# Odd heads' probabilities scaled on GpSimd, and TensorE's queue in the attention ordered by a new model of the engines

## The chip, the cores and the metric

The kernel runs on one core of one Trainium2 chip. The metric is the device time of one execution in microseconds (us); lower is better. A core has TensorE (PE, matrix products), VectorE (DVE), ScalarE (ACT), GpSimd (POOL) and SyncE (SP, which issues most of the transfers here). Each engine executes its own queue in order, and engines wait for one another through semaphores.

## The reference

One decoder layer over 1024 tokens with a width of 1024: RMS norm, one input projection, two token mixers side by side (sparse attention and gated linear attention), a gated merge, an output projection, and a SwiGLU feed-forward block. The change lies in the attention mixer, which does this for each block of 128 queries, each of 8 heads (2 groups of 4):

```python
p_c = masked_softmax(sc, cmp_end[None, :] <= t[:, None])          # compressed keys, 63 of them
o_c = jnp.einsum('bghqn,bgnd->bghqd', p_c.astype(v_cmp.dtype), v_cmp)
...
p_s = masked_softmax(ss, m_s)                                     # selected blocks
o_s = jnp.einsum('bghqm,bgqmd->bghqd', p_s.astype(vs.dtype), vs)
...
p_w = masked_softmax(sw, m_w)                                     # window of 512 tokens
o_w = jnp.einsum('bghqk,bgkd->bghqd', p_w.astype(vwin.dtype), vwin)
gt = lax.dynamic_slice_in_dim(gates, s, Q_BLOCK, axis=3)
return gt[..., 0:1] * o_c + gt[..., 1:2] * o_s + gt[..., 2:3] * o_w
```

With 16 blocks of 64 tokens and 16 selected, every valid block is selected, so the selected branch is causal attention over all earlier tokens.

## The kernel before

**Work of the attention.** A *unit* is one group and one block of 128 queries: first group 0 with i = 7 down to 0, then group 1 with i = 0 up to 7. A unit has two pairs of heads (j = 0, 1). For each pair there is a selected branch (br = 1, `nkb` = i + 1 blocks of 128 keys) and a window branch (br = 2, at most 5 blocks); the compressed branch (br = 0) serves all four heads of the unit at once. The two heads of a pair are called `par` 0 (even) and 1 (odd).

A branch goes through three kinds of steps on TensorE:

- *Scores* (S): products of queries and keys into a PSUM tile `s` (two buffers). DVE adds the mask, writes the probabilities' tile `p` to SBUF (four buffers) and finds the row's extreme (`masked`, line 1135). ACT takes the exponential and sums it (line 1174 for one head, 1162 for a pair). `weigh` then takes the reciprocal of the sum (line 1141) and multiplies `p` by it and by the branch's gate, so that the three branches can be added up in one accumulation. With up to `PAIR` = 4 blocks the two heads are done in one step (`pair_scores`), with more in one step each (`head_scores`).
- *Turns* (T): TensorE transposes up to two blocks of both heads into the PSUM tile `t` (two buffers, line 1210). ACT copies it as the high part `pth` (line 1187), and DVE subtracts that for the low part `ptl` (line 1188).
- *Values* (P): products of both parts with the values into the PSUM tile `o` (line 1219). After a unit's last, `finish` copies the two halves out and adds them on POOL (line 1239).

In `weigh` the even head is scaled on DVE by the reciprocal and the gate in one instruction (line 1149). For the odd head DVE first multiplies reciprocal and gate, 128x1 (line 1146), and ACT then scales `p` (line 1147).

`unit` prepares a unit's rotated queries: a load of the rope table, two shuffles on DVE (1069), three products on POOL (1070 to 1072), four transfers through SP, a copy on ACT (1081) and a subtraction on POOL (1082).

**Fill.** Beside the attention TensorE has independent work, single matmuls of 512 columns (line 431, tile `d`, one PSUM buffer): 14 column tiles of the gate projection, two halves of 24 matmuls each, and 5 tiles of an up-projection, two halves of 12. After a half's last matmul DVE (line 969) or ACT (line 1255) evacuates it. Its weights come from transfers on SP, are split by ACT (372) and POOL (373).

**Order.** TensorE's queue is written out in program order. In the attention `Plan.run` decides that order while the program is built: it keeps a time `t` for TensorE and estimates of when ACT (A), DVE (D) and POOL (P) will be done, and takes at each point a turn, a score or a value step that it holds to be ready, in this order of preference, or else an item of fill. The order of the instructions on the other engines is chosen by the scheduler of the language, from its own simulation. In the old planner each engine has one free time, `on` adds a step to it in the order of the calls, and fill is taken only if nothing of the attention becomes ready within `WAIT` = 300 ns:

```python
if self.fill.q and self.d <= self.t and nxt[0] > self.t + WAIT:
    cost, fn = self.fill.q.popleft()
```

After the plan, what fill is left is issued, and the merge of the two mixers follows (its sigmoid is line 1344).

Of the kernel before, what the change touches and what calls it, by code (L numbers as in the profile page):

```python
# [14 lines left out]
AF = mybir.ActivationFunctionType  # L15
OP = mybir.AluOpType
AX = mybir.AxisListType.X

T, D, DFF = 1024, 1024, 2816
# [86 lines left out]


PAIR, PMAX, PREP = 4, 3, 3
LAT, WAIT, LOADED, COPIED = 155.0, 300.0, 1500.0, 3000.0
NBIG, NMID, NSMALL = 18, 10, 8  # L110
SCRATCH = 2048
FINE, NGATE, AHEAD = 3, 2, 1200

UP = (1, 2, 4, 5, 7)


class Plan:

    def __init__(self, brs, fill, unit):
        self.fill, self.unit = fill, unit
        self.t, self.free = 0.0, dict(A=0.0, D=0.0, P=0.0)
        self.s, self.tb = [0.0] * 2, [0.0] * 2
        self.p = [0.0] * 4
        self.o = self.d = 0.0
        self.turns, self.pend = deque(), deque()
        self.scores = deque()
        self.prep = deque()
        self.known = {}  # L130
        seen = None
        for b in brs:
            if (b.g, b.i) != seen:
                seen = (b.g, b.i)
                self.prep.append((*seen, len(self.scores)))
            for fn, n in b.scores():
                self.scores.append((b, fn, n))
            b.ready = None
            ts = b.turns()
            for k, (fn, n) in enumerate(ts):  # L140
                self.turns.append((b, fn, n, k == len(ts) - 1))
        n = len(self.scores)
        self.prep = deque((g, i, n - k) for g, i, k in self.prep)

    def on(self, eng, ready, dur):
        self.free[eng] = max(self.free[eng], ready + LAT) + dur
        return self.free[eng]

    def prepare(self):
        u = self.prep.popleft()[:2]  # L150
        self.unit(*u)
        t = self.on("D", self.t, 600.0)
        t = self.on("P", t, 2300.0)
        t = self.on("A", t + COPIED, 600.0)
        self.known[u] = self.on("P", t, 1300.0)

    def score_at(self):

        if not self.scores:
            return None  # L160
        b, fn, n = self.scores[0]
        u = (b.g, b.i)
        if self.prep and len(self.scores) <= self.prep[0][2] + PREP:
            self.prepare()
        held = 0 if b.br == 0 else 1
        if len(self.p) < held:
            return None
        return max(self.s[0], self.known[u] if b.br else 0.0)

    def score(self):  # L170
        b, fn, n = self.scores.popleft()
        fn()
        w = 64 if b.br == 0 else 128 * b.nkb
        if b.br == 0:
            cost = 540.0
        else:
            cost = n * 2 * max(107.0, w / 2.4)
        self.t += cost
        self.s.pop(0)
        pf = self.p.pop(0) if b.br else 0.0  # L180
        m = n if b.br else 4
        t = self.on("D", max(self.t, pf), 65 * m + 1.041 * w * m)
        u, t = t, self.on("A", t, m * (237 + 0.833 * w))
        self.s.append((u if b.br else t) + LAT)
        self.s.sort()
        t = self.on("D", t, 150.0)
        t = max(self.on("D", t, 130 + 0.52 * w if b.br else 330.0), self.on("A", t, 187 + 0.833 * w) if b.br and n == 2 else 0.0)
        b.ready = max(b.ready or 0.0, t + LAT)
        b.left = getattr(b, "left", 2) - n

    def turn_at(self):
        if not self.turns or len(self.pend) >= PMAX:
            return None
        b = self.turns[0][0]
        if getattr(b, "left", 2):
            return None
        return max(b.ready, self.tb[0])

    def turn(self):
        b, fn, n, last = self.turns.popleft()  # L200
        later = fn()
        self.t += 218.0 * n
        self.tb.pop(0)
        t = self.on("A", self.t, 50 + 214.0 * n)
        t = self.on("D", t, 68 + 267.0 * n)
        self.tb.append(t + LAT)
        self.tb.sort()
        self.pend.append((t + LAT, later, n, b, last))
        if last and b.br:
            self.p += [self.t + LAT] * (1 if b.nkb <= PAIR else 2)  # L210

    def value_at(self):
        if not self.pend:
            return None
        t, _, _, b, _ = self.pend[0]
        return max(t, self.o) if b.br == 0 and b.j == 0 else t

    def value(self):
        _, later, n, b, last = self.pend.popleft()
        later()  # L220
        self.t += 218.0 * n if b.br else 436.0
        if last and b.br == 2 and b.j == 1:
            self.o = max(self.on("A", self.t, 478.0), self.on("D", self.t, 550.0)) + LAT

    def run(self):
        ops = dict(T=(self.turn_at, self.turn), S=(self.score_at, self.score), P=(self.value_at, self.value))
        while self.scores or self.turns or self.pend:
            at = {k: ops[k][0]() for k in ops}
            now = [k for k in ops if at[k] is not None and at[k] <= self.t]
            if now:  # L230
                ops[now[0]][1]()
                continue
            nxt = min((v, k) for k, v in at.items() if v is not None)
            if self.fill.q and self.d <= self.t and nxt[0] > self.t + WAIT:
                cost, fn = self.fill.q.popleft()
                self.t += cost
                said = fn()
                if said == "pause":
                    self.d = self.on("D", self.t, 670.0) + LAT
                elif said in ("part", "load"):  # L240
                    self.d = self.t + (LOADED if said == "load" else LOADED / 2)
                    self.on("A", self.t + 2500.0, 1040.0)
                continue
            self.t = nxt[0] if not self.fill.q or nxt[0] <= self.t + WAIT else min(nxt[0], self.d)


@with_exitstack
def layer_kernel(ctx, tc, a, outT):
# [135 lines left out]
    def dense(jobs, two=True, per=1, ready=None):  # L384

        w, out = dict(ready or {}), []
        todo = deque((n, o) for n, job in enumerate(jobs) for o in range(0, job[0].shape[1], 4) if (n, o) not in w)
        raw = deque()  # L390

        def fetch():
            if todo:
                n, o = todo.popleft()
                raw.append(((n, o), raw_half(jobs[n][0], o)))

        def load():
            if not raw:
                fetch()
            if raw:  # L400
                at, t = raw.popleft()
                w[at] = half_parts(*t)
            fetch()

        def at(n):
            def getw(k):
                wh, wl = w[n, k // 4 * 4]
                return wh[:, k % 4, :], wl[:, k % 4, :]
            return getw

        out += [(0.0, load if i >= len(w) else lambda: None) for i in range(3)]
        for n in range(len(jobs)):
            items = jobs[n][1](at(n))
            if jobs[n][0].shape[1] > 4:
                cut = (len(items) // 2 if two else 0) + 4 * per
                out += items[:cut] + [(0.0, load)] + items[cut:]
            else:
                out += items
            out.append((0.0, load))
        return out  # L420

    def products(getw, bank, xh, xl, w0, evac, fine=False):

        st, out, n = {}, [], len(xh)

        def at(k, i):
            if k + i == 0:
                st["p"] = bank()
            wh, wl = getw(w0 + k)
            w, x = ((wh, xh[k]), (wh, xl[k]), (wl, xh[k]))[i]  # L430
            PE.matmul(st["p"], w, x, start=k + i == 0, stop=k == n - 1 and i == 2)  # L431
            if k == n - 1 and i == 2:
                evac(st["p"])
                return "pause"

        for k in range(n):
            if fine:
                out += [(216.0, lambda k=k, i=i: at(k, i)) for i in range(3)]
            else:
                out.append((648.0, lambda k=k: [at(k, i) for i in range(3)][2]))  # L440
        return out
# [643 lines left out]
    class Branch:  # L1085
# [51 lines left out]
        def weigh(self, pars, ps, z):  # L1137
# [4 lines left out]
            for i, par in reversed(list(enumerate(pars))):  # L1142
                p, ri, gi = ps[i], r[:, i:i + 1], UN[self.g, self.i]["gt"][:, self.br, h + i:h + i + 1]
                self.p[par] = p
                if par:
                    V.tensor_mul(ri, ri, gi)
                    S.activation(p, p, AF.Copy, scale=ri)
                else:
                    V.tensor_scalar(p, p, ri, gi, op0=OP.mult, op1=OP.mult)

        def pair_scores(self):

# [223 lines left out]
    last = []  # L1376
# [574 lines left out]
```

## Time and profile before

| | |
|---|---|
| time, median of 3 runs | 1565.43 us (1564.54 to 1568.66) |
| the profiled execution | 1564.79 us, span 1563.0 us |
| TensorE, matmul busy | 1542.0 us (99% of the span) |
| DVE / ACT / POOL busy | 1014.2 / 813.0 / 720.4 us (65 / 52 / 46%) |
| granted TensorE clock, mean | 0.998 |
| attention, from the first scores to the last values | about 361 to 762 us |

Busy time is the union of an engine's instructions. Matmuls are pipelined and their ends are modelled, so a short wait of TensorE can lie under the modelled end of the matmul before it; the start times of neighbours show it. A group's row reads: line, engine, operation, tiles written and read, shapes, count | busy us, mean ns of one | idle us of the engine before them, and what ended it. A row of waits reads: who waited <- for whom: us in total, times, longest.

### The profile page before, as it was taken

What the parts mean: (1) busy time and instruction counts of PE and PEld (TensorE: products, weight loads), DVE (VectorE), ACT (ScalarE), POOL (GpSimd) and SP (SyncE); (2) the same over time, 40 slices, a digit from 0 to 9 for tenths busy, and PEclk for the clock granted to TensorE, in tenths of its full rate; (3) what the DMA queues carried; (4) which work ended last, traced back from release to release, by engine and by line L of the source; (5) the groups of instructions that cost most, each with busy time, mean ns of one, the idle gap of its engine ahead of it and who ended that gap; (6) DMA issues with size and microseconds to landing.
All of it is one profiled execution on the core that took longest, in us unless ns stands there. A gap on an engine that the chain in (4) does not pass through costs nothing.

```text
span 1563.0 us, 22871 instructions
## 1 busy us (share of the span) xinstructions
PE 1542.0 (99%) x7871; PEld 1309.6 (84%) x7871; DVE 1014.2 (65%) x1788; ACT 813.0 (52%) x1615; POOL 720.4 (46%) x635
## 2 busy tenths in 40 slices
PE   9999999999999999999999999999999999999998
PEld 7888988888888888888888888888888888888887
DVE  7781487586787778777574677544444444599785
ACT  6241555575776767687653454334333334454542
POOL 6110366573223353343256510666666666555570
PEclk9999999999999999999999999999999999999999
DMA  5431212332111222221656621322222323885422
GB/s 180 139 105 55 69 51 65 119 108 78 48 58 55 77 87 72 85 88 61 200 169 229 197 88 68 121 101 102 101 101 102 101 101 108 299 320 163 141 88 108
DMA packets 109944, 180.15 MB, mean 115 GB/s; under 512 B 13426, under 2 KB 30595, under 8 KB 109828
## 3 DMA queue, kind: packets, MB, share of 16 engines
q1 hardware_dynamic: 105796, 172.25, 33.4%
q10 hardware_dynamic: 4032, 6.44, 1.1%
q8 instruction: 62, 1.02, 0.3%
q14 instruction: 54, 0.44, 0.1%
HBM read 128.57 MB, written 45.88 MB: 112 GB/s over the span
## 4 chain that ended last, share of the span: by engine, by line
PE 93%; DVE 3%; ACT 1%; issue 1%; POOL 0%; DVEq 0%; POOLq 0%; ACTq 0%
PE m L431 19%; PE d L431 11%; PE m L1494 9%; PE m L1492 9%; PE m L1493 9%; PE m L1880 5%; PE m L1882 4%; PE m L1881 4%; PE t L1210 3%; PE o L1219 3%; PE s L1130 2%; PE s L1129 2%; PE t L749 2%; PE t L750 1%; PE t L751 1%; PE t L884 1%
## 5 line engine op out<-in xcount | busy, mean ns | idle before, releaser
L373 POOL TENSOR_TENSOR wl<-wf,wh 128x512 fp32r<-128x512 f32 x106 | 146.5, 1389 | 260.7 <-ACT wh L372 237.4
L1492 PE MATMUL m<-xt,wh 128*128 128x512 f32 x412 | 160.3, 389 | 0.0
L1493 PE MATMUL m<-xt,wh 128*128 128x512 f32 x412 | 160.3, 389 | 0.0
L1494 PE MATMUL m<-xt,wl 128*128 128x512 f32 x412 | 160.3, 389 | 0.0
L1409 POOL TENSOR_TENSOR wl<-ws,wh 128x512 fp32r<-128x512 f32 x76 | 107.6, 1420 | 73.3 <-ACT wh L1408 73.3
L1188 DVE TENSOR_TENSOR ptl<-t,pth 128x512 fp32r<-128x512 f32 (+1 forms) x168 | 99.2, 597 | 42.7 <-ACT pth L1187 40.5
L1409 POOL TENSOR_TENSOR wl<-wr,wh 128x512 fp32r<-128x512 f32 x69 | 92.0, 1333 | 70.3 <-ACT wh L1408 69.3
L1408 ACT ACTIVATE wh<-wr 128x512 fp32r<-128x512 f32 x87 | 55.0, 632 | 121.3 <-POOL wl L1409 89.1
L1408 ACT ACTIVATE wh<-ws 128x512 fp32r<-128x512 f32 x76 | 48.0, 632 | 131.4 <-PE m L1493 113.8
L1187 ACT ACTIVATE pth<-t 128x512 fp32r<-128x512 f32 (+1 forms) x168 | 86.4, 519 | 53.0 <-PE t L1210 43.7
L1880 PE MATMUL m<-xb,wh 128*128 128x512 f32 x280 | 109.1, 389 | 0.3 <-DVE g L1554 0.3
L1409 POOL TENSOR_TENSOR wl<-wd,wh 128x512 fp32r<-128x512 f32 x56 | 81.9, 1465 | 59.1 <-ACT wh L1408 57.7
L1881 PE MATMUL m<-xb,wh 128*128 128x512 f32 x280 | 109.0, 389 | 0.0
L1882 PE MATMUL m<-xb,wl 128*128 128x512 f32 x280 | 108.9, 389 | 0.0
L1409 DVE TENSOR_TENSOR xb<-ar,xb 128x512 fp32r<-128x512 f32 x73 | 82.3, 1146 | 29.0 <-ACT xb L1408 29.0
L431 PE MATMUL m<-hh,wh 128*128 128x512 f32 x240 | 99.9, 416 | 0.1
L372 ACT ACTIVATE wh<-wf 128x512 fp32r<-128x512 f32 x106 | 66.1, 626 | 61.1 <-PE m L431 19.9
L1135 DVE CUSTOM_DVE_ANT_0 p<-s,qz 128x640 f32<-128x640 f32 (+7 forms) x128 | 86.3, 700 | 12.8 <-PE s L1130 12.5
L431 PE MATMUL m<-hh,wl 128*128 128x512 f32 x240 | 93.8, 391 | 0.0
L431 PE MATMUL m<-hl,wh 128*128 128x512 f32 x240 | 93.6, 390 | 0.0
L1210 PE MATMUL t<-ident,p 128*128 128x128 f32 x528 | 83.9, 275 | 8.4 <-DVE ptl L1188 6.1
L1493 PEld LDWEIGHTS m<-xt,wh 128*128 128x128 f32 x412 | 77.4, 188 | 16.2
(402 smaller groups left out, 4506.4 us busy)
## 6 DMA issues: line engine op xcount, KB each, us to landing
ar<-actd SPq DMA_DIRECT2D x77, 256.0 KB, 2.8
wf<-in_w_t SPq DMA_DIRECT2D x58, 256.0 KB, 2.8
wr<-in_w_gate SPq DMA_DIRECT2D x44, 256.0 KB, 2.8
wr<-in_w_upf SPq DMA_DIRECT2D x44, 256.0 KB, 2.7
wd<-in_w_down SPq DMA_DIRECT2D x33, 256.0 KB, 5.2
zd<-zt SPq DMA_DIRECT2D x32, 256.0 KB, 2.0
zz<-zd SPq DMA_DIRECT2D x16, 512.0 KB, 4.7
wf<-in_w_out SPq DMA_DIRECT2D x32, 256.0 KB, 3.3
```

Of the source, the lines that this page charges most:

```text
L373: P.tensor_tensor(tl, wf, f(th), OP.subtract)
L431: PE.matmul(st["p"], w, x, start=k + i == 0, stop=k == n - 1 and i == 2)
L1188: V.tensor_tensor(tl[:, :c], pt[:, :c], f(th[:, :c]), OP.subtract)
L1210: PE.transpose(pt[:, bs(2 * b + par)], self.p[par][:, bs(kb + b)], ident)
L1408: S.activation(th, src, AF.Copy)
L1409: eng.tensor_tensor(tl, src, f(th), OP.subtract)
L1492: PE.matmul(ps, wh[:, c], xh, start=first and k == 0, stop=False, skip_group_check=not first)
L1493: PE.matmul(ps, wh[:, c], xl, start=False, stop=False, skip_group_check=not first)
L1494: PE.matmul(ps, wl[:, c], xh, start=False, stop=k == MH - 1, skip_group_check=not first)
L1880: PE.matmul(dst, wh[:, c], xh, start=first and p == 0, stop=False, skip_group_check=not first)
L1881: PE.matmul(dst, wh[:, c], xl, start=False, stop=False, skip_group_check=not first)
L1882: PE.matmul(dst, wl[:, c], xh, start=False, stop=p == NP - 1, skip_group_check=not first)
```

## The change

Two things. In `weigh`, the odd head's probabilities are multiplied by reciprocal and gate in one instruction on POOL, with the same form that the even head has on DVE; ACT's scaling and DVE's small product are gone. And `Plan` has a new model: every instruction group of ACT, DVE and POOL is a `Step` with predecessors; `advance` runs each engine's waiting steps, the earliest issued of those that are ready first; `over` tells whether a step has ended by now. Its durations are new, steps of a pair are counted one head at a time, and loads of weights put work on ACT and POOL. Fill is taken as soon as no attention step is ready, and a group of fill with fewer than `CLOSE` = 6 matmuls left goes ahead of the attention.

```diff
-LAT, WAIT, LOADED, COPIED = 155.0, 300.0, 1500.0, 3000.0
+LAT, TAIL, LOADED, COPIED = 100.0, 320.0, 1500.0, 3000.0
+CLOSE = 6
...
-    def on(self, eng, ready, dur):
-        self.free[eng] = max(self.free[eng], ready + LAT) + dur
-        return self.free[eng]
+    def step(self, eng, dur, *after, lag=LAT):
+        self.n += 1
+        s = Step(dur, 0.0, self.n)
+        for x in after:
+            if not isinstance(x, Step):
+                s.at = max(s.at, x + lag)
+            elif x.end is not None:
+                s.at = max(s.at, x.end + lag)
+            else:
+                x.outs.append((s, lag, eng))
+                s.left += 1
+        if not s.left:
+            self.wait[eng].append(s)
+        return s
+
+    def advance(self, t):
+        while True:
+            best = None
+            for e, w in self.wait.items():
+                if w:
+                    at = max(self.free[e], min(s.at for s in w))
+                    if at < t and (best is None or at < best[0]):
+                        best = at, e
+            if best is None:
+                return
+            at, e = best
+            s = min((s for s in self.wait[e] if s.at <= at), key=lambda s: s.seq)
+            self.wait[e].remove(s)
+            s.end = self.free[e] = at + s.dur
+            for x, lag, eng in s.outs:
+                x.at, x.left = max(x.at, s.end + lag), x.left - 1
+                if not x.left:
+                    self.wait[eng].append(x)
+
+    def over(self, x):
+        if isinstance(x, Step):
+            return x.end is not None and x.end + LAT <= self.t
+        return x <= self.t
...
     def score(self):
...
-        m = n if b.br else 4
-        t = self.on("D", max(self.t, pf), 65 * m + 1.041 * w * m)
-        u, t = t, self.on("A", t, m * (237 + 0.833 * w))
-        self.s.append((u if b.br else t) + LAT)
-        self.s.sort()
-        t = self.on("D", t, 150.0)
-        t = max(self.on("D", t, 130 + 0.52 * w if b.br else 330.0), self.on("A", t, 187 + 0.833 * w) if b.br and n == 2 else 0.0)
...
+            m = [self.step("D", 232.0 + 1.043 * w, self.t, pf, lag=TAIL) for _ in range(n)]
+            self.s.append(m[-1])
+            zs = [self.step("A", 469.0 + 0.851 * w, x) for x in m]
+            r = self.step("D", 160.0, *zs)
+            par = getattr(b, "par", 0)
+            if n == 2 or par:
+                b.steps.append(self.step("P", 100.0 + 1.05 * w, r))
+            if n == 2 or not par:
+                b.steps.append(self.step("D", 270.0 + 0.53 * w, r, lag=0.0))
+            b.par = par + 1
...
     def turn(self):
...
-        t = self.on("A", self.t, 50 + 214.0 * n)
-        t = self.on("D", t, 68 + 267.0 * n)
+        t = self.step("A", 165.0 + 214.0 * n, self.t, lag=TAIL)
+        t = self.step("D", 151.0 + 268.0 * n, t)
...
     def run(self):
...
+            self.advance(self.t)
+            now = next((do for ok, do in ops if ok()), None)
+            if now and not (self.fill.q and getattr(self.fill.q[0][1], "left", CLOSE) < CLOSE and self.over(self.d)):
+                now()
                 continue
-            nxt = min((v, k) for k, v in at.items() if v is not None)
-            if self.fill.q and self.d <= self.t and nxt[0] > self.t + WAIT:
+            if self.fill.q and self.over(self.d):
                 cost, fn = self.fill.q.popleft()
                 self.t += cost
                 said = fn()
...
+                elif said == "weights":
+                    self.step("P", 1292.0, self.step("A", 630.0, self.t + 2500.0))
...
-            self.t = nxt[0] if not self.fill.q or nxt[0] <= self.t + WAIT else min(nxt[0], self.d)
+            self.t += 25.0
...
-                if par:
-                    V.tensor_mul(ri, ri, gi)
-                    S.activation(p, p, AF.Copy, scale=ri)
-                else:
-                    V.tensor_scalar(p, p, ri, gi, op0=OP.mult, op1=OP.mult)
+                (P if par else V).tensor_scalar(p, p, ri, gi, op0=OP.mult, op1=OP.mult)
```

More of the change, by code (lines that the diff above doesn't have):

```diff
@@ L108, with __init__ @@
 PAIR, PMAX, PREP = 4, 3, 3
-LAT, WAIT, LOADED, COPIED = 155.0, 300.0, 1500.0, 3000.0
+LAT, TAIL, LOADED, COPIED = 100.0, 320.0, 1500.0, 3000.0
 NBIG, NMID, NSMALL = 18, 10, 8
 SCRATCH = 2048
+CLOSE = 6
 FINE, NGATE, AHEAD = 3, 2, 1200
 UP = (1, 2, 4, 5, 7)
+class Step:
+    __slots__ = ("dur", "left", "at", "outs", "end", "seq")
+    def __init__(self, dur, at, seq):
+        self.dur, self.at, self.seq = dur, at, seq
+        self.left, self.outs, self.end = 0, [], None
 class Plan:
@@ L122, in __init__ @@
         self.fill, self.unit = fill, unit
-        self.t, self.free = 0.0, dict(A=0.0, D=0.0, P=0.0)
+        self.t, self.n = 0.0, 0
+        self.free, self.wait = dict(A=0.0, D=0.0, P=0.0), dict(A=[], D=[], P=[])
         self.s, self.tb = [0.0] * 2, [0.0] * 2
@@ L137, in __init__ @@
                 self.scores.append((b, fn, n))
-            b.ready = None
+            b.steps, b.left = [], 2
             ts = b.turns()
@@ L151, in prepare, with score_now @@
         self.unit(*u)
[L152 to L157, printed above, removed]
+        t = self.step("D", 600.0, self.t)
+        t = self.step("P", 2230.0, t)
+        t = self.step("A", 630.0, t, lag=COPIED)
+        self.known[u] = self.step("P", 1295.0, t)
+    def score_now(self):
         if not self.scores:
-            return None
+            return False
         b, fn, n = self.scores[0]
@@ L164, in score_at @@
             self.prepare()
[L165 to L168, printed above, removed]
+        if len(self.p) < (0 if b.br == 0 else 1):
+            return False
+        return any(self.over(x) for x in self.s) and (not b.br or self.over(self.known[u]))
     def score(self):
@@ L173, in score, with turn_now @@
         w = 64 if b.br == 0 else 128 * b.nkb
+        self.t += 540.0 if b.br == 0 else n * 2 * max(108.0, w / 2.4 + 13)
+        self.s.remove(next(x for x in self.s if self.over(x)))
         if b.br == 0:
-            cost = 540.0
-        else:
[L177 to L180, printed above, removed]
-        m = n if b.br else 4
-        t = self.on("D", max(self.t, pf), 65 * m + 1.041 * w * m)
-        u, t = t, self.on("A", t, m * (237 + 0.833 * w))
-        self.s.append((u if b.br else t) + LAT)
-        self.s.sort()
-        t = self.on("D", t, 150.0)
-        t = max(self.on("D", t, 130 + 0.52 * w if b.br else 330.0), self.on("A", t, 187 + 0.833 * w) if b.br and n == 2 else 0.0)
-        b.ready = max(b.ready or 0.0, t + LAT)
-        b.left = getattr(b, "left", 2) - n
-    def turn_at(self):
+            t = self.step("D", 414.0, self.t, lag=TAIL)
+            e = self.step("A", 2056.0, t)
+            self.s.append(e)
+            t = self.step("D", 178.0, e)
+            t = self.step("D", 446.0, t, lag=0.0)
+            b.steps.append(self.step("D", 426.0, t, lag=0.0))
+        else:
+            pf, zs = self.p.pop(0), []
+            m = [self.step("D", 232.0 + 1.043 * w, self.t, pf, lag=TAIL) for _ in range(n)]
[8 more added lines that the diff above has]
+            b.par = par + 1
+        b.left -= n
+    def turn_now(self):
         if not self.turns or len(self.pend) >= PMAX:
-            return None
+            return False
         b = self.turns[0][0]
-        if getattr(b, "left", 2):
-            return None
-        return max(b.ready, self.tb[0])
+        return not b.left and all(self.over(x) for x in b.steps) and any(self.over(x) for x in self.tb)
     def turn(self):
@@ L202, in turn, with value_now @@
         self.t += 218.0 * n
-        self.tb.pop(0)
-        t = self.on("A", self.t, 50 + 214.0 * n)
-        t = self.on("D", t, 68 + 267.0 * n)
-        self.tb.append(t + LAT)
-        self.tb.sort()
-        self.pend.append((t + LAT, later, n, b, last))
+        self.tb.remove(next(x for x in self.tb if self.over(x)))
+        t = self.step("A", 165.0 + 214.0 * n, self.t, lag=TAIL)
+        t = self.step("D", 151.0 + 268.0 * n, t)
+        self.tb.append(t)
+        self.pend.append((t, later, n, b, last))
         if last and b.br:
-            self.p += [self.t + LAT] * (1 if b.nkb <= PAIR else 2)
-    def value_at(self):
+            self.p += [self.t] * (1 if b.nkb <= PAIR else 2)
+    def value_now(self):
         if not self.pend:
-            return None
+            return False
         t, _, _, b, _ = self.pend[0]
-        return max(t, self.o) if b.br == 0 and b.j == 0 else t
+        return self.over(t) and (b.br > 0 or b.j > 0 or self.over(self.o))
     def value(self):
@@ L220, in value @@
         later()
-        self.t += 218.0 * n if b.br else 436.0
+        self.t += 238.0 * n if b.br else 480.0
         if last and b.br == 2 and b.j == 1:
-            self.o = max(self.on("A", self.t, 478.0), self.on("D", self.t, 550.0)) + LAT
+            a, d = self.step("A", 596.0, self.t, lag=TAIL), self.step("D", 682.0, self.t, lag=TAIL)
+            self.o = self.step("P", 1460.0, a, d)
+            self.o = d
     def run(self):
-        ops = dict(T=(self.turn_at, self.turn), S=(self.score_at, self.score), P=(self.value_at, self.value))
+        ops = ((self.turn_now, self.turn), (self.score_now, self.score), (self.value_now, self.value))
         while self.scores or self.turns or self.pend:
[L228 to L231, printed above, removed]
+            self.advance(self.t)
+            now = next((do for ok, do in ops if ok()), None)
+            if now and not (self.fill.q and getattr(self.fill.q[0][1], "left", CLOSE) < CLOSE and self.over(self.d)):
+                now()
                 continue
-            nxt = min((v, k) for k, v in at.items() if v is not None)
-            if self.fill.q and self.d <= self.t and nxt[0] > self.t + WAIT:
+            if self.fill.q and self.over(self.d):
                 cost, fn = self.fill.q.popleft()
@@ L238, in run @@
                 if said == "pause":
-                    self.d = self.on("D", self.t, 670.0) + LAT
+                    self.d = self.step("D", 687.0, self.t, lag=TAIL)
+                elif isinstance(said, float):
+                    self.d = self.t + said
+                elif said == "weights":
+                    self.step("P", 1292.0, self.step("A", 630.0, self.t + 2500.0))
                 elif said in ("part", "load"):
                     self.d = self.t + (LOADED if said == "load" else LOADED / 2)
-                    self.on("A", self.t + 2500.0, 1040.0)
+                    for _ in range(2):
+                        self.step("P", 1292.0, self.step("A", 630.0, self.t + 2500.0))
                 continue
-            self.t = nxt[0] if not self.fill.q or nxt[0] <= self.t + WAIT else min(nxt[0], self.d)
+            self.t += 25.0
 @with_exitstack
@@ L403, in load @@
             fetch()
+            return "weights"
         def at(n):
@@ L437, in products, with fn @@
             if fine:
-                out += [(216.0, lambda k=k, i=i: at(k, i)) for i in range(3)]
+                for i in range(3):
+                    def fn(k=k, i=i):
+                        return at(k, i)
+                    fn.left = 3 * (n - k) - i
+                    out.append((216.0, fn))
             else:
```

## The prediction

> **What bounds the kernel now.** I read the view of cores first, then the chain that ended last.
>
> ```profile
> core 0: 1563.0 us, clock 0.998
> ```
> ```profile
> PE 93%; DVE 3%; ACT 1%; issue 1%; POOL 0%; DVEq 0%; POOLq 0%; ACTq 0%
> ```
>
> TensorE (PE) bounds the whole. The change touches only its waits in the attention, about 357 to 762.3 us, so next come the busy times of three stretches of it, and TensorE's waits.
>
> ```profile
> 752.50:762.30 9.80, 7.07 (x46) 6.81 (x45) 3.10 (x5) 6.01 (x9) 1.28 (x1) 0.83 0.71 232
> 700.00:752.50 52.50, 51.21 (x324) 45.45 (x324) 39.27 (x90) 41.19 (x85) 15.64 (x16) 1.00 0.19 65
> 357.00:752.50 395.50, 389.57 (x2385) 344.37 (x2384) 292.82 (x819) 282.39 (x695) 139.64 (x141) 1.00 0.22 70
> ```
> ```profile
> PE t L1210 <- DVE ptl L1188: 6.1, 10, 2.7
> PE t L1210 <- ACT p L1147: 1.4, 1, 1.4
> PE t L1210 <- DVE rr L1141: 0.7, 2, 0.4
> PE d L431 <- DVE zt L969: 0.2, 1, 0.2
> ```
>
> The columns are the length, then busy time of PE, its loads, DVE, ACT and POOL, then clock and DMA. PE idles 5.9 us in the first 395.5 and 2.7 in the last 9.8; DVE, ACT and POOL are busy 74, 71 and 35% of the long stretch. Modelled ends of matmuls hide short waits, so I also count the work at the pitch of dense pieces: the chain in order of time, then the timeline.
>
> ```profile
> 579.32 5.47 PE d L431 x24
> ...
> 586.20 0.44 PE s L1108 x4
> 586.75 0.24 PE d L431
> 586.99 0.44 PE t L1210 x4
> 587.42 0.24 PE o L1219 x2
> ```
> ```profile
> 538.40 0.28 PE L1130 MATMUL s<-ks,qs 128*128 128x256 f32 x1
> 538.52 0.28 PE L1129 MATMUL s<-ks,qs 128*128 128x256 f32 x1
> ```
> ```profile
> 357.00:752.50 395.50, 201.38 (x813) 147.50 (x811) 1.00 0.22 70
> 700.00:752.50 52.50, 20.56 (x84) 15.29 (x84) 1.00 0.19 65
> ```
> ```profile
> L1210 PE MATMUL t<-ident,p 128*128 128x128 f32 x528 | 83.9, 275 | 8.4 <-DVE ptl L1188 6.1 <-ACT p L1147 1.4 <-DVE rr L1141 0.7
> L1219 PE MATMUL o<-pth,vs 128*128 128x256 f32 x264 | 66.0, 319 | 0.0
> ```
>
> The third fence is the fill (line 431) alone. Fill: 814 x 0.228 (5.47/24) = 185.6 us. Transposes: 528 and, by the loops, 32 compressed, x 0.11 = 61.6. Value products: two parts, 528, and 64 compressed, x 0.12 = 71.0. Scores: the loops give 33,792 columns of odd heads (8 or fewer blocks for the selected branch, 5 for the window, two pairs of heads, two groups), as many even, two parts each: 135,168 columns, 0.12 per 256, 63.4. Compressed scores: 64 x 0.11 and 16 biases x 0.12, 8.9. Together 390.5 of 405.3, so **about 15 us can be recovered**, 0.9% of the kernel. The last 9.8 us hold 46 matmuls, about 5.3 us of work: 4.5 lost there, 10.3 before it.
>
> **The change part by part.** First the rows of what moves: two groups, two single lines, and POOL's.
>
> ```profile
> L1147 ACT ACTIVATE p<-p,rr 128x1024 f32<-128x1024 f32 (+7 forms) x64 | 46.9, 732 | 8.0 <-DVE rr L1146 7.4 <-DVE p L1149 0.3
> ...
> L1146 DVE TENSOR_TENSOR rr<-rr,gz 128x1 f32<-128x1 f32 x64 | 15.6, 244 | 1.4
> ```
> ```profile
> L1146 DVE TENSOR_TENSOR rr<-rr,gz x64: 140/159/1182, 373.2 to 751.0; 128x1 f32<-128x1 f32 x64
> ```
> ```profile
> L1149 DVE TENSOR_SCALAR p<-p,rr,gz x64: 332/611/1562, 372.3 to 749.7; 128x640 f32<-128x640 f32 x20, 128x512 f32<-128x512 f32 x8, 128x384 f32<-128x384 f32 x8, 128x256 f32<-128x256 f32 x8
> ```
> ```profile
> L1082 POOL TENSOR_TENSOR qs<-qq,qs 128x512 fp32r<-128x512 f32 x16 | 20.7, 1295 | 54.8 <-ACT qs L1081 54.8
> ...
> L1296 POOL CAST oah<-oa 128x512 fp32r<-128x512 f32 x4 | 2.6, 676 | 0.1
> ```
>
> *Odd heads to GpSimd (POOL).* ACT loses 64 x 0.732 = 46.9 us, a sixth of its work; DVE loses 64 x 0.244 = 15.6. POOL gains 64 scalings of 528 columns on average. No row shows POOL scaling by two scalars. Nearest below is the cast (one tensor read): 676 x 528/512 = 0.70 us, 44.6 in all. Above is the subtraction of two tensors: 1.34 us, 85 in all. I take the cast, because the new instruction too reads one tensor; POOL then stands near 185 of 405 us. A gain on TensorE's path comes only from waits on ACT. The one wait on line 1147, 1.4 us, goes: ACT ran an odd head behind an exponential there. Late next are POOL's earlier entries. On an idle POOL an odd head is ready 0.03 + 0.24 us sooner; a POOL that is 35% busy with pieces of 0.7 to 1.3 us gives back some 0.2. I set that at 0.
>
> [...]
>
> [...] Line 1149 took up to 1562 ns against a median of 611, line 1146 up to 1182 against 159. In pairs of heads (four blocks or fewer, 32 pairs) POOL's scaling and DVE's now start from the same reciprocal. If one waits for the other, DVE loses up to 32 x 0.42 us (320 columns on average) = 13.5, about what line 1146 gave back (15.6). I take 0; both ends, -15.6 and +13.5, lie on a DVE that is 74% busy.
>
> [...]
>
> *The planner's durations.* ACT's and DVE's dearest shapes:
>
> ```profile
> L1187 ACT ACTIVATE pth<-t 128x512 fp32r<-128x512 f32 x112 | 65.7, 590 | 37.3 <-PE t L1210 36.8
> L1174 ACT ACTIVATE p<-p,nm 128x640 f32<-128x640 f32 x40 | 32.9, 824 | 10.7 <-DVE nm L1135 10.3 <-issue 0.3
> ```
> ```profile
> L1188 DVE TENSOR_TENSOR ptl<-t,pth 128x512 fp32r<-128x512 f32 x112 | 76.5, 687 | 39.6 <-ACT pth L1187 37.8
> L1135 DVE CUSTOM_DVE_ANT_0 p<-s,qz 128x640 f32<-128x640 f32 x40 | 31.8, 817 | 7.2 <-PE s L1130 7.1
> ```
>
> The old planner counts 478 for the copy that measured 590, 602 for the subtraction of 687, 731 for the mask of 817, and nothing for ACT's scaling of a single head. The new one counts 593, 687 and 899 (with the mask's accumulator). From a turn's transposes to its bank being free it reckons 320 + 593 + 100 + 687 + 100 = 1800 ns, where the old had 155 + 478 + 155 + 602 + 155 = 1545: 255 ns more, about one fill matmul put ahead of the next turn. The nine waits on line 1188 before the last 10 us come to 6.1 - 2.7 = 3.4 us, 0.38 each; 255 ns takes over half of such a wait. The old rule also idled rather than start fill within 300 ns of the next attention step; the new one starts fill at once. I take half of the early loss that neither lines 1147, 1141 nor 969 explain: (10.3 - 1.4 - 0.9)/2 = 4.0 us. Bounds: 8.0 if all goes, below nothing if waits form elsewhere (the rivals).
>
> *Closing a fill group.* With five or fewer matmuls left, fill goes ahead: an attention step stands up to 5 x 0.228 = 1.1 us later. No work is added; the other branch in flight covers it. Without that cover it is up to 1.1 us for each of the 38 groups (28 of 24 matmuls, 10 of 12).
>
> *Moved with the order:* each unit's rope load, two shuffles, three POOL products, four copies through memory, ACT copy and POOL subtraction; the weight loads with a split on ACT and POOL; evacuations and their stores on SP's queue. The same in number, at nothing: DMA is at 0.22 and a unit is still prepared three scores ahead. Uncovered, each of 16 units would show at least its subtraction, 1.3 us.
>
> *The last 10 us.* Timelines of ACT and PE:
>
> ```profile
> 753.16 1.28 ACT L1344 ACT_TABLE_LOAD   x1
> 754.46 1.06 ACT L1344 ACTIVATE zz<-zz 128x1024 f32<-128x1024 f32 x1
> 755.42 0.58 ACT L1255 ACTIVATE zt<-d 128x512 f32<-128x512 f32 x1
> 755.90 1.07 ACT L1187 ACTIVATE pth<-t 128x512 fp32r<-128x512 f32 x2
> ```
> ```profile
> 757.27 0.70 PE L1210 MATMUL t<-ident,p 128*128 128x128 f32 x4 [2.73 <-DVE ptl L1188]
> ```
>
> The fill is out, and ACT serves the next stage's sigmoid ahead of the turns; nothing in the change moves that, so 0, between -4.5 (fill left over) and the third rival's loss.
>
> **Sum:** 1.4 + 4.0 = 5.4 us off the profiled execution (span 1563.0, time 1564.79): 1559.4. That execution lies 0.64 under the median, so **1560.0** against 1565.43.
>
> **Rivals.** The measurement can tell 0.3%, 4.7 us, from no change: 1560.7 to 1570.1.
>
> *No change: relief off the path.* For it: ACT is only 71% busy and one wait in 14 names line 1147; many of the ptl waits are DVE's own queue, and other waits appear when fill moves. It gives 1564 if only line 1147's wait goes. Against: the old planner's short durations are on the very chain that waits.
>
> *Slower: POOL's queue.*
>
> ```profile
> POOL qs L1082 <- ACT qs L1081: 54.8, 13, 8.8
> POOL oa L1239 <- DVE fp L1236: 51.6, 9, 13.9
> ```
>
> POOL executes in order and stood 4.2 us on average behind a query part that was not there yet, 5.7 behind an output's sum. Odd heads queued behind such an entry arrive that late, and with them the turn. To pass +4.7 it must undo 5.4 as well: 10.1 us, three such hits uncovered out of 64; three cost 12.6, which ends 7.2 above before, 1572.6. Against: line 1082 stood at POOL's head with nothing else queued; order among the engines other than PE is the scheduler's.
>
> *Slower: fill runs out early.* Longer durations spend fill sooner. From 700 to 752.5 fill is 84 x 0.228 = 19 us; without it 33 us of attention would be paced by DVE's and ACT's 39 to 41, 6 to 8 lost. The last 10 us lost half. Between these, 30 us bare at a third lost cost some 11 against the sum: 1571. Against: work saved from waits lets attention run on as well.
>
> [...]
>
> **How the numbers follow.** The forecast case 0.46 (1552 to 1560.7), no change 0.32, POOL's queue 0.12, fill 0.06, port 0.04. Faster 0.46, same 0.32, slower 0.22. A range from 1554 to 1573 leaves out about 0.08 below and 0.11 above; the forecast case alone would be 1554 to 1560.7.
>
> **What the profile after would show.** POOL's scalings of 512 columns near 0.68 us; ACT 47 us and line 1146 gone; transposes waiting for line 1188 in the first 395 us down from 3.4 to under 2; the attention's end near 757. Wrong if transposes wait for POOL's p, if scalings take over 1 us, if the last fill stands tens of us before the end, or if PE's idle time merely has other names.

## The result, and the profile after

| | before | after |
|---|---|---|
| time, median | 1565.43 us (1564.54 to 1568.66) | 1582.22 us (1580.82 to 1585.18) |
| ratio to before, 95% interval | | 1.0104 (1.009 to 1.0119) |
| span of the profiled execution | 1563.0 us | 1583.2 us |
| first scores to the merge's first matmul, in the trace | 361.5 to 762.1: 400.6 us | 365.3 to 781.9: 416.6 us |

The kernel became 16.8 us slower; 1560.0 had been forecast, with a range that ended at 1573. The attention stage with the fill that belongs to it grew by 16.0 us, which is nearly all of the loss. (The other 4 us between the two spans lie before it: in this one trace the granted clock was 0.54 from 69.0 to 76.5 us, where the trace of before has 1.00, and the first scores start 3.8 us later. In the other kernels' traces below they start between 360.7 and 363.9.)

First each engine's share of the chain that ended last, then TensorE's waits in the stage, of the changed kernel:

```profile
PE 87%; DVE 5%; POOL 2%; issue 2%; DMA 2%; ACT 1%; SPq 0%; DVEq 0%; POOLq 0%; ACTq 0%
```
```profile
PE o L1257 <- DVE fp L1291: 9.4, 9, 3.0
PE d L486 <- POOL obl L1332: 4.0, 2, 2.7
PE o L486 <- POOL obl L1332: 2.4, 2, 2.0
PE t L1265 <- DVE ptl L1243: 1.2, 2, 1.0
PE t L1265 <- POOL p L1204: 0.9, 1, 0.9
PE d L486 <- DVE zt L1028: 0.6, 1, 0.6
```

TensorE's share of the chain fell from 93 to 87%. The waits of before are nearly gone: transposes waited 6.1 us for DVE's `ptl` (line 1188, now 1243), now 1.2. Two kinds of wait stand there that before did not have, beside one of 0.9 us for POOL's `p`: for `fp`, and for `obl`.

**The first: the accumulator's bank, 9.4 us in nine waits.** A unit's compressed values (line 1257) open the bank `o` anew, and must wait until ACT's `fo` and DVE's `fp` have copied the last unit's sum out of it. Timelines of ACT, DVE and PE around the longest one; the last value product of the old unit ends at 517.54.

```profile
519.01 0.59 ACT L1287 ACTIVATE fo<-o 64x512 f32<-64x512 f32 x1
```
```profile
521.43 0.68 DVE L1291 COPY fp<-o 64x512 f32<-64x512 f32 x1
```
```profile
522.16 0.50 PE L1257 MATMUL o<-pth,vc 128*128 128x256 f32 x2 [2.99 <-DVE fp L1291]
...
523.48 0.63 PE L486 MATMUL d<-hl,wh 128*128 128x512 f32 x1
523.91 0.63 PE L486 MATMUL d<-hh,wl 128*128 128x512 f32 x1
```

ACT comes to `fo` 1.5 us after the values, `fp` starts 1.8 us after `fo` has ended, and TensorE, with only 1.6 us of other work put in between, stands for 2.99. From 523.48 on, 1.3 us after the pause, eight matmuls of 512 columns start 0.43 us apart, where the pitch is 0.228: the granted clock is 0.52 from 523.5 to 526.9 us, where it was 1.00 from 361 to 523.3, and that is another 1.6 us. Of the nine waits only this one and one of 2.70 us are followed by such a spell (0.50 from 543.9 to 547.2).

The planner calls the bank free when `fp` is done and lets `fo` and `fp` run side by side (`self.o = d`); in the traces of before and after `fp` never starts sooner than 0.03 us after `fo` has ended, in any of the 15 units. But this alone is not what the change brought: the old planner had the two side by side as well (the later of 478 ns on ACT and 550 on DVE). What differs, by the code, is that the old one put each copy behind everything issued to its engine before it, and the new one only behind steps that are ready. In the traces `fo` begins no later than it did (1.25 us after a unit's last values before, 1.27 after, as means over 15 units), and `fp` 0.26 and 0.53 us after `fo` has ended. TensorE comes sooner: it had 1.6 to 9.8 us of other work between a unit's last values and the next compressed values, 4.7 on average, and now has 1.4 to 4.7, 2.9 on average.

**The second: fill behind the attention.** The last value product starts at 735.15, where it was at 762.01. The attention runs 27 us ahead, and 161 of the 792 fill matmuls are left. This is the stretch from there to the merge, then the low parts `obl` of the operands of the up-projection, after and before:

```profile
735.20:782.00 46.80, 40.36 (x164) 31.81 (x164) 8.27 (x8) 15.33 (x28) 26.50 (x22) 0.93 0.68 218
```
```profile
L1332 POOL TENSOR_TENSOR obl<-obf,obh x8: 1254/1290/1727, 735.1 to 755.9; 128x512 fp32r<-128x512 f32 x8
```
```profile
L1277 POOL TENSOR_TENSOR obl<-obf,obh x8: 1281/1294/1309, 662.2 to 683.4; 128x512 fp32r<-128x512 f32 x8
```

164 matmuls at 0.228 would take 37 us; they took 46.8, at a clock of 0.93. In the queue of before the eight splits `obl` ran under the attention. Now they come up only at its end, from 735.1 on, and on POOL they meet the splits of the attention's output and of weights. The chain that ended last, in this stretch alone, goes through POOL:

```profile
by line: PE t L486 21.3%; POOL obl L1332 21.3%; PE o L486 17.4%; PE d L486 14.2%; POOL oal L1352 10.5%; issue 6.8%; POOL oah L1351 4.7%; POOL wl L427 3.9%; POOLq L1332 0.1%
```

So of the 30.6 us that the stage loses against its work (416.6 less the 390.5 counted before, of which 4.5 lie ahead of the first scores), about 10 are lost behind the attention and 20 in it. Before, it was 14.6: 4.5 in the last 10 us and 10 ahead of them. Of the 16 us that were added, then, some 5 lie at the end and some 11 in the attention. In the attention the waits listed above come to 12.1 us and the two spells of lower clock to some 3; the other 5 of the 20 stand in no list of waits, as about 5 of the 10 before stood in none. The odd heads' scaling itself:

```profile
L1204 POOL TENSOR_SCALAR p<-p,rr,gz 128x1024 f32<-128x1024 f32 (+7 forms) x64 | 53.2, 831 | 145.1 <-DVE rr L1200 125.1
```
```profile
L1204 DVE TENSOR_SCALAR p<-p,rr,gz x64: 327/613/1599, 379.7 to 724.8; 128x640 f32<-128x640 f32 x20, 128x512 f32<-128x512 f32 x8, 128x384 f32<-128x384 f32 x8, 128x256 f32<-128x256 f32 x8
```

It took 831 ns on average where 700 had been estimated from the cast (ACT took 732), 53.2 us in all, between the two bounds of 44.6 and 85. Scalings of 512 columns took 936, and 680 had been expected. The even heads on DVE keep their median (613 against 611) and their rare maximum (1599 against 1562).

### The profile page after: what moved, and what is told of

Its sections match the earlier page's. It is cut to its first block, busy times and chain, and to the rows that moved or that the text cites. A ratio compares the mean times of both kernels' runs of the same rounds, so it can differ in the third digit from the quotient of the medians.

```text
span 1583.2 us, 22839 instructions
## 1 busy us (share of the span) xinstructions
PE 1550.0 (98%) x7871; PEld 1314.4 (83%) x7871; DVE 1010.4 (64%) x1724; ACT 773.2 (49%) x1551; POOL 771.9 (49%) x699
## 4 chain that ended last, share of the span: by engine, by line
PE 87%; DVE 5%; POOL 2%; issue 2%; DMA 2%; ACT 1%; SPq 0%; DVEq 0%; POOLq 0%; ACTq 0%
PE m L486 17%; PE m L1547 9%; PE m L1549 9%; PE m L1548 9%; PE d L486 8%; PE m L1935 4%; PE m L1936 4%; PE m L1937 4%; PE o L1274 3%; PE t L1265 3%; PE s L1189 2%; PE s L1188 2%; PE t L808 2%; PE t L810 1%; PE t L809 1%
## 5 line engine op out<-in xcount | busy, mean ns | idle before, releaser
L1204 POOL TENSOR_SCALAR p<-p,rr,gz 128x1024 f32<-128x1024 f32 (+7 forms) x64 | 53.2, 831 | 145.1 <-DVE rr L1200 125.1
L1194 DVE CUSTOM_DVE_ANT_0 p<-s,qz 128x640 f32<-128x640 f32 (+7 forms) x128 | 86.3, 700 | 15.1 <-PE s L1189 14.6
L1549 PEld LDWEIGHTS m<-xt,wl 128*128 128x128 f32 x412 | 77.4, 188 | 16.1
```

The lines of the kernel that those rows point to most:

```text
L1549: PE.matmul(ps, wl[:, c], xh, start=False, stop=k == MH - 1, skip_group_check=not first)
```

## The experiments

Theory 1: the new order of TensorE's queue costs the time (1a by fill behind the attention, 1b by compressed values placed too early). Theory 2: POOL's scaling costs it, by its length, its place in POOL's queue, or by holding up DVE's instructions beside it.

| | edit | time, us | ratio to before, 95% | stage, us |
|---|---|---|---|---|
| e1 | POOL's scaling, old planner | 1560.95 | 0.9962 (0.9949 to 0.9975) | 396.7 |
| e2 | ACT's scaling, new planner | 1585.82 | 1.0125 (1.011 to 1.014) | 420.2 |
| e4 | after, no late operands | 1571.05 | 1.0026 (1.0015 to 1.0038) | 407.3 |
| e3 | after, copies serial in the planner | 1571.42 | 1.0043 (1.0029 to 1.0056) | 403.9 |
| e9 | e3 and e4 together | 1565.44 | 1.0000 (0.9989 to 1.0011) | 398.6 |
| e5 | after, fill paced | 1566.28 | 1.0000 (0.999 to 1.0009) | 401.4 |
| e6 | e5, copies serial | 1566.85 | 1.0010 (1.0 to 1.0021) | 399.8 |
| e10 | e5, POOL at its measured price | 1566.88 | 1.0006 (0.9995 to 1.0016) | 399.6 |
| e11 | e5, closing rule off | 1578.08 | 1.0083 (1.0066 to 1.01) | 413.7 |

The stage is that of the first table, in each kernel's own trace. Before had medians of 1566.37, 1565.47 and 1565.2 beside e1, e2, e4, e5; e3, e9, e6; and e10, e11. The changed kernel was not measured again beside them; differences from its 1582.22, and between groups, are of medians taken apart. In e4 and e9 operands are left out, so that their result differs.

**The two halves of the change, each alone (e1, e2).** In e1 the kernel before gets this edit only; in e2 the changed kernel loses it.

```diff
-                if par:
-                    V.tensor_mul(ri, ri, gi)
-                    S.activation(p, p, AF.Copy, scale=ri)
-                else:
-                    V.tensor_scalar(p, p, ri, gi, op0=OP.mult, op1=OP.mult)
+                (P if par else V).tensor_scalar(p, p, ri, gi, op0=OP.mult, op1=OP.mult)
```

> The kernel before with one edit: odd heads are scaled on POOL as in the change; the old planner and so TensorE's old queue stay. Theory 1 (the loss of 16.8 us comes from the new order of TensorE's queue): 1561 to 1570, near the 1565.4 of before; transposes may wait a little longer for POOL's p. [...]

> The changed kernel with one edit taken back: odd heads are scaled as before, by DVE's small product and ACT; the new planner stays as it is, so TensorE's queue is that of the changed kernel. Theory 1 (order): 1577 to 1588, with the compressed branch's value products waiting for DVE's fp and fill left over after the attention. Theory 2 (POOL): 1570 or less, since the odd heads no longer stand behind POOL.

POOL's scaling alone makes the kernel 5.4 us faster; the order alone makes it 19.5 slower. By the traces, TensorE's queue in e1 has the order of before, and in e2 that of the changed kernel. Theory 2, which had e1 at 1575 or more, falls: in either order POOL's scaling is the better one (5.4 us in the old; 3.6 in the new, 1585.82 to 1582.22, not measured side by side). TensorE's waits in the stage, of e1 and then of e2:

```profile
PE t L1206 <- DVE ptl L1184: 5.1, 6, 3.2
PE d L431 <- DVE zt L969: 0.7, 1, 0.7
```
```profile
PE o L1261 <- DVE fp L1295: 12.4, 9, 2.7
PE o L486 <- POOL obl L1336: 3.0, 2, 1.9
PE d L486 <- POOL obl L1336: 2.6, 2, 1.5
PE t L1269 <- DVE ptl L1247: 2.3, 3, 2.0
PE t L1269 <- ACT p L1206: 2.3, 1, 2.3
```

In e1 the waits for ACT's `p` and for the reciprocal are gone, those for `ptl` ahead of the last one fell from nine with 3.4 us to five with 1.9, and no wait names POOL. In e2 both new waits stand there without any scaling on POOL.

**Late operands (e4).** The up-projection uses heads 0 and 1 of the linear attention in place of 2 and 3, whose loads and splits are left out; TensorE's queue is unchanged in order and number.

```diff
         for h in (2 * hp, 2 * hp + 1):
+            if hp:
+                if hf == 0:
+                    obh.append(obh[h - 2])
+                    obl.append(obl[h - 2])
+                continue
```

> The changed kernel, with the operands of the up-projection for heads 2 and 3 of the linear attention not loaded and not split (heads 0 and 1 are used in their place, which changes the result); TensorE's queue keeps its order and its number of matmuls. In the changed kernel 161 fill matmuls stand behind the attention, and TensorE waits there 6.4 us in four waits for POOL's obl and then runs some 14 matmuls at the lower clock. Theory 1a (these operands come late because the attention that used to cover their loads is over): the waits go, 7 to 11 us faster than the changed kernel, 1571 to 1575. Rival (fill behind the attention is bound by its weights' loads or splits anyway): within 3 us of 1582.

```profile
732.20:768.80 36.60, 36.60 (x164) 30.32 (x163) 7.54 (x8) 12.75 (x24) 20.80 (x18) 1.00 0.63 223
```

11.2 us faster than the change. The same 164 matmuls behind the attention now take 36.6 us with no idle time at a clock of 1.00, against 46.8 at 0.93. So the fill left over cost nothing by itself here; what cost was its late operands. Whether their loads or their splits come last, e4 does not tell apart; the chain above names the splits on POOL.

**The copies one after the other (e3), and both (e9).**

```diff
-            a, d = self.step("A", 596.0, self.t, lag=TAIL), self.step("D", 682.0, self.t, lag=TAIL)
-            self.o = self.step("P", 1460.0, a, d)
-            self.o = d
+            a = self.step("A", 596.0, self.t, lag=TAIL)
+            self.o = self.step("D", 682.0, a)
+            self.step("P", 1460.0, self.o)
```

> The changed kernel with one edit in the planner: the accumulator's bank counts as free when DVE's copy fp is done after ACT's copy fo, one after the other, where the changed planner lets them run side by side (in every trace so far fp starts 0.03 us or more after fo has ended). TensorE's queue then holds 3.1 to 7.0 us of other work between a unit's last values and the next unit's compressed values, where the changed kernel has 1.3 to 4.8; behind the attention 120 fill matmuls are left in place of 161. Theory 1b (the planner's side-by-side copies put compressed values too early): the 9.4 us of waits for fp go to under 3, and with them the spells of lower clock; the loss behind the attention stays: 1570 to 1575. Rival (DVE is late for other reasons, the planner's place is not the matter): waits for fp over 6 us, 1578 or more.

> Both suspects taken from the changed kernel at once: the serial copies in the planner (as in the run before this one) and no loads and splits of heads 2 and 3's operands (heads 0 and 1 in their place, which changes the result). If the two causes add up, 11 us from the operands and 8 to 12 from fp: 1559 to 1564, at or under the 1560.95 of the old order with POOL's scaling. If a third cause matters, 1567 or more.

```profile
PE t L1265 <- DVE ptl L1243: 4.7, 9, 1.8
PE d L486 <- DVE zt L1028: 3.1, 3, 2.2
PE t L1265 <- POOL p L1204: 2.5, 2, 1.6
PE o L1274 <- ACT pth L1242: 1.7, 1, 1.7
```

These are e3's first four waits in the stage. No wait for `fp` is left, and the time fell by 10.8 us, as expected; but not by that way alone. With more fill in between only 120 matmuls are left behind the attention, the operands come under it, and the waits for `obl` vanish as well; in exchange other waits grew. So e3 doesn't price the bank alone, and the two edits of e9 do not add up: 1565.44, 6.0 us under e3, where 1559 to 1564 had been expected. Beside e4 the serial copies bring only 5.6 us (1571.05 to 1565.44), in place of 10.8: a price between these is all that can be said of the bank. Together the two edits take back the loss. In e3 ACT's copies of the operands, ahead of their splits, stand among the last turns instead.

**A pace for the fill (e5, e6).**

```diff
-            if now and not (self.fill.q and getattr(self.fill.q[0][1], "left", CLOSE) < CLOSE and self.over(self.d)):
+            close = self.fill.q and getattr(self.fill.q[0][1], "left", CLOSE) < CLOSE
+            if now and not (self.fill.q and (close or self.late()) and self.over(self.d)):
...
+    def late(self):
+        work = sum(n for _, _, n, _ in self.turns)
+        if self.work is None:
+            self.work = work
+        return FILLS - self.filled > FILLS * work / self.work
```

> The changed kernel with a pace for the fill: in the planner a fill matmul goes ahead of a ready attention step while the share of fill left is larger than the share of turns left, so that no fill is left behind the attention (14 attention matmuls come after the last fill). Theory 1a: the 8 to 11 us lost behind the attention go; the 9.4 us of waits for fp may stay or shrink, as more fill stands between: 1562 to 1574. Theory 2 (POOL): still 1578 or more, since every scaling is as late as it was.

> The changed kernel with the fill paced and the copies serial in the planner; nothing is left out of the computation. Paced alone came to 1566.28 with 2.8 us of waits on the accumulator's bank and 4.6 on turns. Theory 1: the waits for fp go and no fill is left: 1560 to 1566. If the paced queue loses elsewhere (turns placed too early, since fill no longer goes where attention waits): 1566 to 1572.

```profile
PE t L1276 <- DVE ptl L1254: 3.7, 4, 1.9
PE o L1285 <- ACT pth L1253: 2.0, 1, 2.0
PE t L1276 <- POOL p L1215: 0.9, 1, 0.9
PE o L1268 <- DVE fp L1302: 0.8, 2, 0.6
```

This is e5. The pace alone takes back 15.9 of the 16.8 us, and with the loss behind the attention the waits for `fp` go too, from 9.4 to 0.8, though the planner still has the copies side by side. By the starts in the traces, ACT began `fo` 1.27 us after a unit's last values in the changed kernel and 0.60 in e5, as means over 15 units: with fill between the attention's steps ACT is less behind. e6, with the copies in series as well, gains nothing (1566.85). It missed the 1560 to 1566 of its first case and fell to the second, that the paced queue loses elsewhere.

**Two rules of the paced planner (e10, e11).**

```diff
-                b.steps.append(self.step("P", 100.0 + 1.05 * w, r))
+                b.steps.append(self.step("P", 385.0 + 0.8 * w, r))
```
```diff
-CLOSE = 6
+CLOSE = 0
```

> The paced kernel, with POOL's scaling in the planner at the price that the trace of the changed kernel shows (487 ns for 128 columns, 877 for 640, 1203 for 1024: 385 + 0.8 per column, in place of 100 + 1.05). The paced order with POOL's scaling is 5 us slower than the old order with it (1566.28 against 1560.95). Theory A (turns are placed too early because the planner takes POOL for faster than it is): the wait for POOL's p (0.9 us) and some waits for ptl go, 1562 to 1565. Rival (its price is not the matter): 1565 to 1568.

> The paced kernel without the rule that a fill group with fewer than six matmuls left goes ahead of the attention. Theory B (closing a group holds attention steps back and costs time): 1562 to 1565. Rival (the rule costs nothing, since some fill has to be issued anyway): within 2 us of 1566.3.

POOL's price in the planner is not the matter, as far as this edit tests it: TensorE's queue differs from e5's in a few places only. The closing rule is worth some 12 us in the paced order, contrary to both expectations. These are e11's first waits in the stage:

```profile
PE d L497 <- DVE zt L1039: 10.3, 11, 2.9
PE o L1268 <- DVE fp L1302: 2.9, 3, 1.7
```

The fill has one bank, and a group's first matmul stands until DVE has evacuated the group before it: 10.3 us against 0.6 in e5. By the traces an evacuation begins 0.82 us after its group's last matmul on average, and 0.25 in e5. Why the paced order stays 5 us behind the old order with the same scaling (1566.28 against 1560.95) was not settled; its waits on turns and values, 6.6 us, are spread over many places.

## Why the prediction was wrong

- **The work to be recovered, 15 us:** nothing speaks against the count, and for the fill it was borne out: e4's 164 matmuls without idle time took 36.6 us, and 37 by the counted pitch. The rest of it was not measured again.
- **Odd heads to POOL:** right in sign, and its rival (POOL's queue) did not happen: 0.9 us in one wait. ACT's wait on line 1147 went. The price was 831 ns where the cast had given 700. The forecast put 1.4 us on this half of the change; alone it gave 5.4, with the stage 3.9 shorter in the traces. In e1, without the new planner, the waits for `ptl` before the last turns fell from 3.4 to 1.9: part of what I had credited to the planner came with POOL's scaling.
- **DVE beside POOL:** near the 0 that was taken. 15.6 us of line 1146 went, and DVE's busy time fell by 3.8 (1014.2 to 1010.4): the even heads' scalings took 2.6 us more than before, the compressed branch's product `ec` 4.4 and the split `oal` 3.6 (in e2, without POOL's scaling, it grew as well). What lengthened them was not tested. In the trace of before, line 1146 took 140 to 162 ns in the 50 places with no POOL instruction beside it and 563 on average in the 14 with one; the longest, 1182 at 464.31, ended 14 ns after POOL's split of weights (line 373). That a port is behind it, to which the list of chances gives 0.04, no run shows; in place of a loss of up to 13.5 us on DVE the runs showed 2.6 in the even heads' scalings, and waits on `ptl` that fell from 6.1 to 1.2.
- **The planner's durations, "255 ns more, about one fill matmul put ahead of the next turn", 4.0 us:** the term that failed. Waits on `ptl` before the last turns did fall, from 3.4 to 1.2, but I took one chain's sum for the order's whole effect. The order alone made the kernel 19.5 us slower (e2). It put less fill among the attention's steps and not more: 161 matmuls fewer. The bank of the accumulator was not priced at all: 9.4 us of waits, and two spells of lower clock behind them. What in the new model brings the attention's steps forward was not isolated; that a step no longer stands behind all that was issued before it is read from the code.
- **The last 10 us, "so 0, between -4.5 (fill left over) and the third rival's loss":** this failed too. Fill left over was taken for a gain, because I counted its matmuls and not what it issues: loads, ACT's copies and POOL's splits, which the attention had covered. It cost 10 us behind the attention in place of the 4.5 lost there before.
- **Closing a fill group, moved steps at nothing:** closing helps (e11). The moved steps belong to the failed one before this: "a unit is still prepared three scores ahead" looked at the units, and not at the fill's own operands.
- **The rivals:** fill running out early had the wrong sign, the attention ran ahead by 27 us where the forecast had it end near 757. Slower with 0.22 was too little, and the upper end, 1573, came from a rival whose price I had found for other reasons.

e1 beats both kernels: POOL's scaling in the old order.

## What to carry to other kernels

When a queue is rearranged, follow what each item issues on the other engines: an item moved behind the work that hid its loads and splits shows them in full, although its own work is the same. An "attention first, fill into the gaps" order is only as good as the times its model gives: here the new ones let the chain run ahead and left fill for the end. Pacing the fill by the share of work done took back nearly all of the loss, with no better model. Test a change that joins a new operation and a new order by its halves first: here they had opposite signs.

## What the runs showed of the hardware

In these traces some pauses of TensorE cost more than their length. Behind the one of 2.99 us eight matmuls of 512 columns started 0.43 us apart at a granted clock of 0.52, and 0.228 is the pitch at 1.00. In e5 the same followed a shorter one, of 1.85 us:

```profile
703.11 0.44 PE L1276 MATMUL t<-ident,p 128*128 128x128 f32 x2 [1.85 <-DVE ptl L1254]
703.31 0.63 PE L497 MATMUL d<-obh,wh 128*128 128x512 f32 x1
703.73 0.63 PE L497 MATMUL d<-obl,wh 128*128 128x512 f32 x1
```

Not every pause does. In e6 the same transposes waited 1.86 us, at 704.09, and the clock stayed at 1.00 (the third number from the end); e5 first, then e6:

```profile
700.00:712.00 12.00, 10.15 (x55) 8.73 (x55) 7.04 (x15) 6.79 (x20) 8.58 (x9) 0.86 0.21 69
```
```profile
700.00:712.00 12.00, 10.14 (x68) 9.15 (x68) 8.38 (x20) 7.91 (x23) 10.19 (x11) 1.00 0.27 88
```

What decides between the two, no run here shows.

GpSimd's multiplication by two per-row scalars took 487 ns for 128 columns, 877 for 640 and 1203 for 1024 on average, some 385 ns and 0.8 ns per column: a higher start and a lower slope than the planner's 100 and 1.05. The line does not hold for all: those of 512 columns, where both heads of a pair are scaled at once, took 763 to 1057, 936 on average and so more than those of 640. The runs do not show why.
